# Attention heads in pairs on different rows and columns of the PE array, with a pair's transposes in two PSUM banks

## The chip, the cores and the metric

One core of a Trainium2 chip runs the whole program. The metric is the device time of one execution in microseconds (us); lower is better. TensorE is called PE here, VectorE DVE, ScalarE ACT, GpSimd POOL, and SP issues the loads of weights.

## What is computed

One sequence of 256 tokens with 1024 features goes through two kinds of layers, two of each. The first kind is an FFN, a mixer and an FFN; the mixer has 8 NSA query heads in 2 groups that share keys and values (three branches each: compressed blocks, selected blocks, a window), and 8 MoBA heads. At this length the selected blocks and the window both come to causal attention over all 256 keys. The second kind is a hybrid mixer (8 sparse heads, 4 differential heads) and an FFN. All heads have 64 features. The core of the mixer, cut:

```python
for l in range(DEPTH):
    x = x + 0.5 * swiglu(rms_norm(x, norm_ffn1[l]), ...)
    x = x + hybrid_mixer(rms_norm(x, norm_mix[l]), w_in[l], ...)
    x = x + 0.5 * swiglu(rms_norm(x, norm_ffn2[l]), ...)

def nsa_mixer(q, k_cmp, v_cmp, k_slc, v_slc, k_win, v_win, gates, ...):
    ...
    p_w = masked_softmax(s_w, valid_w)
    o_win = jnp.einsum('bgrcqk,bgckd->bgrcqd', p_w, vw)
    return g[..., 0:1] * o_cmp + g[..., 1:2] * o_slc + g[..., 2:3] * o_win
...
return jnp.concatenate([o_nsa, o_moba], axis=-1) @ w_out
```

The differential heads take `softmax(q0 k0) - lam * softmax(q1 k1)` times v; the sparse heads have a mask from an indexer that keeps 64 keys a query.

## The kernel before

Every projection is a float32 product made of three passes (lines 201 to 206, `mm3`): both operands are split into a high and a low part, weights by ACT and DVE (L183, L184) in chunks of 1 MB. Eight PSUM banks are shared by tag: four `acc` (projections, and the sums of `to_residual`, which takes all four), two `S` (`psS`, scores), one `T` (`psT`, transposes), one `O` (`psO`, outputs). A planner takes the program's instructions by their place in it: on each engine it issues the earliest one whose operands and bank it holds to be ready, so that products of a later projection run between those of the heads. PE then works through that order and waits where an operand is late.

An attention stage works on two heads at a time (a pair). `scores_exp` (L361 to 383) makes, for one head after the other in a bank of its own: the scores of the late 128 queries with 256 keys (L371), those of the early ones with 128 keys (L372), and two products with a bfloat16 identity that add the mask (L373, L374); then DVE takes a maximum (L377) and ACT an exponential with its sum (L380), twice a head. `attend` (L399 to 413) scales the probabilities (L405, L406) and then, for one head after the other, makes three transposes into the one `psT` bank (L389 to 391, `p_T`), copies them to SBUF (ACT for the first head, L394, DVE for the second, L396) and makes the two products with the values into 64 of the rows of `psO` (L412, L413). A float32 product with the heads' operands goes to PE as two instructions.

The mixer (L432 to 571) has this program order: the projection of keys and values, windows, queries, `moba_in(0)` (MoBA's queries), the compressed branch (`cmp_probs`), then `nsa(k)` for k = 0 to 3 (two `attend` each, and a product with the compressed values, L533), `moba_in(1)`, the transposes of MoBA's queries (`heads_T`, L350), `moba_in(2)`, the transposes of its keys, `moba(k)` four times, and `to_residual` with `w_out` (L242 to 246). NSA's pair is two query heads of one group, both on the same 64 rows; MoBA's pair is two heads on rows 0 to 63 and 64 to 127.

The hybrid (L816 to 1116) goes: indexer, queries, keys, the differential queries, `av`, then `sparse(k)` four times (L1007), the projection of the differential keys (`xc`), `bv`, `diff(h)` four times (L1019; it has `scores_exp` and one `p_T`, and products L1034 to 1036), the gates' products (`gate`, L964) into `acc`, and the up-projections.

Of the kernel before, what the change touches and what calls it, by code (L numbers as in the profile page):

```python
# [9 lines left out]
F32 = mybir.dt.float32  # L10
# [10 lines left out]
D = 1024  # L21
# [11 lines left out]
class K:  # L33
    """One core's program: two macaron layers (NSA and MoBA mixer), then two layers of the
    sparse and differential hybrid. Tokens lie on partitions in the residual and in the
    attention inputs, features on partitions where a product contracts them."""
# [6 lines left out]
    # ---------------------------------------------------------------- set-up  # L43
# [49 lines left out]
    def loads(self):  # L93
        """What later stages want from DRAM beside their weights."""
# [25 lines left out]
    def more_consts(self):  # L120
# [3 lines left out]
        self.caus = cp.tile([128, 128], BF16, name="caus")  # L124
# [3 lines left out]
            pattern=[[-1, 128]], channel_multiplier=1,  # L128
# [61 lines left out]
    # ---------------------------------------------------------------- norms  # L190
    def rstd_of(self, ms, n, tag):
        """(ms / n + EPS) ** -0.5"""
        nc = self.nc
        w = ms.shape[-1]
        v = self.small(w, tag + "v")
        nc.gpsimd.tensor_scalar(v, ms, 1.0 / n, EPS, op0=ALU.mult, op1=ALU.add)
        r = self.small(w, tag + "r")
        nc.gpsimd.tensor_tensor(r, v, self.neghalf[:, 0:w], op=ALU.pow)
        return r

    def mm3(self, out, ah, al, bh, bl, start, stop):
        """out += (ah + al).T @ (bh + bl); al.T @ bl lies below float32's own rounding."""
# [5 lines left out]
    def behind(self, ins):  # L208
        """What is traced within queues behind these instructions, each on its engine."""
# [10 lines left out]
    def ft(self):  # L220
        """A bank for a tile of features; leaves the accumulators of to_residual alone."""
# [3 lines left out]
    # ------------------------------------------------ products to the residual  # L225
    def to_residual(self, yh, yl, w, nk, scale, after, held=2):
        """x += scale * y @ w, y with features on partitions (yh(k), yl(k): [128, 256]). The early
        tokens end first, and after(t, n) is told of each piece of x."""
# [20 lines left out]
        for c in range(nch):  # L249
            hl = self.weights(  # L250
                w[c * 256 : (c + 1) * 256, :].rearrange("(j p) n -> p j n", p=128), [2, D]
            )
# [12 lines left out]
    # ------------------------------------------------------------------ FFN  # L265
# [77 lines left out]
    def heads_T(self, pool, src, name, scale=None):  # L343
        """src [128, 2, 512] (8 heads of 64) -> [128, 4, 256]: two heads on each column of tiles."""
# [16 lines left out]
    def scores_exp(self, pool, qk, masks):  # L361
        """Two heads: exp(s - max) [128, 2, 384] (late queries first), sums [128, late or early x head]."""
        nc = self.nc
        m1, m0 = masks
# [3 lines left out]
        for i, (q, k) in enumerate(qk):  # L368
            ps = self.psS()
            w = m1.shape[-1]  # L370
            nc.tensor.matmul(ps[:, 0:256], q[:, 128:256], k[:, 0:256], start=True, stop=False)  # L371
            nc.tensor.matmul(ps[:, 256:384], q[:, 0:128], k[:, 0:128], start=False, stop=False)  # L372
            nc.tensor.matmul(ps[:, 256 - w : 256], self.identb, m1, start=False, stop=False)  # L373
            nc.tensor.matmul(ps[:, 256:384], self.identb, m0, start=False, stop=True)  # L374
            for t, c0, c1 in ((0, 0, 256), (1, 256, 384)):
                j = 2 * t + i
                nc.vector.tensor_reduce(  # L377
                    nm[:, j : j + 1], ps[:, c0:c1], axis=AX.X, op=ALU.max, negate=True
                )
                nc.scalar.activation(  # L380
                    p[:, i, c0:c1], ps[:, c0:c1], AF.Exp, bias=nm[:, j : j + 1], accum_out=sm[:, j : j + 1]
# [3 lines left out]
    def p_T(self, pool, p, eng):  # L385
        """[128, 384] -> keys on partitions: [k0 x q0 | k0 x q1 | k1 x q1]"""
        nc = self.nc
        ps = self.psT()
        nc.tensor.transpose(ps[:, 0:128], p[:, 256:384], self.ident)  # L389
        nc.tensor.transpose(ps[:, 128:256], p[:, 0:128], self.ident)  # L390
        nc.tensor.transpose(ps[:, 256:384], p[:, 128:256], self.ident)
        pt = pool.tile([128, 384], F32, tag="PT", name="PT", bufs=3)
        if eng == 0:
            nc.scalar.copy(pt, ps[:, 0:384])  # L394
        else:
            nc.vector.tensor_copy(pt, ps[:, 0:384])  # L396
        return pt

    def attend(self, pool, o, qk, vs, masks, coef, start, stop):  # L399
        """o [2 heads x 64, 256] += softmax(q k) v, rows weighted by what coef makes of the sums."""  # L400
        nc = self.nc
        p, sm = self.scores_exp(pool, qk, masks)
        c = coef(sm)
        for i in range(2):
# [26 lines left out]
    # ------------------------------------------------------------ first mixer  # L431
    def mixer(self, l, pr, after):  # L432
# [3 lines left out]
        with tc.tile_pool(name="mix", bufs=1) as mp, ExitStack() as es:  # L436
# [13 lines left out]
            vcb = mp.tile([128, 2, 256], F32, name="vcb")  # L450
# [51 lines left out]
            caus = (self.caus, self.caus)  # L502

            def gated(h, i):
                def coef(sm):
# [3 lines left out]
                    cv = c.rearrange("p (t h) -> p t h", t=2)  # L509
                    gv = gt.rearrange("p t (h i) -> p t h i", i=3)  # L510
                    for t in (1, 0):
                        nc.vector.tensor_tensor(
                            cv[:, 1 - t, :], cv[:, 1 - t, :], gv[:, t, h : h + 2, i], op=ALU.mult
# [10 lines left out]
            def nsa(k):  # L524
                g = k // 2
                gs = slice(64 * g, 64 * g + 64)
                o = self.psO()
                for i, v in ((1, kv[:, :, 384 + 64 * g : 448 + 64 * g]), (2, kw[:, :, 128 + 64 * g : 192 + 64 * g])):
                    qk = [(qrT[gs, (2 * k + j) % 4, :], kT[i - 1][gs, :]) for j in range(2)]
                    vs = [[v[:, t, :] for t in range(2)]] * 2  # L530
                    self.attend(mp, o, qk, vs, caus, gated(2 * k, i), start=i == 1, stop=False)
                kk = (2 * k) % 4
                nc.tensor.matmul(  # L533
                    o[:, 0:256], vcb[:, g, kk * 64 : kk * 64 + 128], pcT[:, g, :], start=False, stop=True
# [786 lines left out]
```

## Time and profile before

| | us |
|---|---|
| median of three runs | 1950.57 (1947.41 to 1956.95) |
| span of the profiled execution | 1950.2 |
| the profiled execution's own time | 1950.2 (its span; no other time stands for it) |
| PE busy | 1906.6 (98%), 12336 matrix instructions |
| PE weight loads | 1676.6 (86%), beside the products |
| DVE busy | 1250.6 (64%) |
| ACT busy | 922.4 (47%) |
| POOL busy | 327.1 (17%) |
| chain that ended last | PE 90%, DVE 5%, POOL 2% |
| a 1 MB chunk of weights, from issue to landing | 4.8 to 5.1 (medians by weight) |

The ends of PE's instructions are modelled, and each lasts longer than it holds the array up, so that PE reads as busy almost throughout. What an instruction costs a stretch without gaps is the distance from its start to the next one's.

### The profile page before, as it was taken

What the parts mean: (1) busy time and instruction counts of PE and PEld (TensorE: products, weight loads), DVE (VectorE), ACT (ScalarE), POOL (GpSimd) and SP (SyncE); (2) the same over time, 40 slices, a digit from 0 to 9 for tenths busy, and PEclk for the clock granted to TensorE, in tenths of its full rate; (3) what the DMA queues carried; (4) which work ended last, traced back from release to release, by engine and by line L of the source; (5) the groups of instructions that cost most, each with busy time, mean ns of one, the idle gap of its engine ahead of it and who ended that gap; (6) DMA issues with size and microseconds to landing.
All of it is one profiled execution on the core that took longest, in us unless ns stands there. A gap on an engine that the chain in (4) does not pass through costs nothing.

```text
span 1950.2 us, 30625 instructions
## 1 busy us (share of the span) xinstructions
PE 1906.6 (98%) x12336; PEld 1676.6 (86%) x12336; DVE 1250.6 (64%) x2138; ACT 922.4 (47%) x1664; POOL 327.1 (17%) x360
## 2 busy tenths in 40 slices
PE   8999999999999999999999998999999989999999
PEld 8998776899899988767999775899998767999997
DVE  6764475665657655666666487766765696666662
ACT  6553354544445444445444453545444534545442
POOL 4110120011102101100111154000210351011110
PEclk9999999999999999899999998999999999999999
DMA  8545452354655364612546443355546532355552
GB/s 277 191 166 186 163 204 68 108 174 152 216 183 185 130 237 153 216 44 87 177 162 224 157 140 108 109 178 189 174 137 215 191 115 104 124 179 174 173 194 88
DMA packets 149023, 314.63 MB, mean 161 GB/s; under 512 B 5525, under 2 KB 30257, under 8 KB 148881
## 3 DMA queue, kind: packets, MB, share of 16 engines
q1 hardware_dynamic: 147952, 311.15, 47.0%
q0 software_dynamic: 896, 1.52, 0.4%
q8 instruction: 97, 1.59, 0.3%
q14 instruction: 46, 0.37, 0.1%
q10 hardware_dynamic: 32, 0.01, 0.0%
HBM read 311.61 MB, written 1.05 MB: 160 GB/s over the span
## 4 chain that ended last, share of the span: by engine, by line
PE 90%; DVE 5%; POOL 2%; issue 1%; DMA 1%; ACT 1%; SPq 0%; POOLq 0%; ACTq 0%; DVEq 0%
PE acc L205 12%; PE acc L206 12%; PE acc L204 11%; PE acc L243 8%; PE acc L246 8%; PE acc L242 8%; PE psS L204 3%; PE psS L205 3%; PE psS L206 3%; PE psS L371 3%; PE psT L204 2%; PE psT L206 2%; PE psT L205 2%; PE psO L412 2%; PE psO L204 1%; PE psO L206 1%
## 5 line engine op out<-in xcount | busy, mean ns | idle before, releaser
L184 DVE TENSOR_TENSOR lo<-raw,hi 128x1024 fp32r<-128x1024 f32 (+1 forms) x604 | 708.8, 1197 | 374.1 <-ACT hi L183 372.6
L183 ACT ACTIVATE hi<-raw 128x1024 fp32r<-128x1024 f32 (+1 forms) x604 | 584.6, 1007 | 458.5 <-PE acc L205 134.0
L205 PE MATMUL acc<-xl,hi 128*128 128x256 f32 x1408 | 400.2, 285 | 0.0
L204 PE MATMUL acc<-xh,hi 128*128 128x256 f32 x1408 | 399.2, 285 | 0.0
L206 PE MATMUL acc<-xh,lo 128*128 128x256 f32 x1408 | 398.7, 284 | 0.0
L205 PEld LDWEIGHTS acc<-xl,hi 128*128 128x128 f32 x1408 | 271.0, 192 | 0.4
L204 PEld LDWEIGHTS acc<-xh,hi 128*128 128x128 f32 x1408 | 270.3, 193 | 0.5 <-ACT xh L1222 0.2
L206 PEld LDWEIGHTS acc<-xh,lo 128*128 128x128 f32 x1408 | 270.0, 192 | 0.0
L312 POOL TENSOR_TENSOR hh<-sg,gu 128x256 f32<-128x256 f32 x132 | 139.0, 1059 | 650.5 <-DVE sg L308 626.4
L243 PE MATMUL acc<-lo,gh 128*128 128x512 f32 x528 | 210.7, 399 | 0.0
L242 PE MATMUL acc<-hi,gh 128*128 128x512 f32 x528 | 208.4, 395 | 0.0
L205 PE MATMUL acc<-lo,xh 128*128 128x512 f32 (+2 forms) x416 | 164.6, 396 | 13.9 <-DVE lo L184 13.9
L246 PE MATMUL acc<-hi,gl 128*128 128x512 f32 x528 | 173.9, 396 | 0.0
L204 PE MATMUL acc<-hi,xh 128*128 128x512 f32 (+2 forms) x416 | 163.3, 396 | 2.4 <-ACT ix L854 1.9
L206 PE MATMUL acc<-hi,xl 128*128 128x512 f32 (+2 forms) x416 | 162.3, 392 | 2.7 <-DVE xl L1223 2.7
L204 PE MATMUL psS<-xh,hi 128*128 128x256 f32 x480 | 136.6, 285 | 0.0
L206 PE MATMUL psS<-xh,lo 128*128 128x256 f32 x480 | 136.0, 283 | 0.0
L205 PE MATMUL psS<-xl,hi 128*128 128x256 f32 x480 | 136.0, 283 | 0.0
L217 ACT ACTIVATE gh<-hh 128x256 fp32r<-128x256 f32 x132 | 55.2, 418 | 149.2 <-POOL hh L312 149.0
L243 PEld LDWEIGHTS acc<-lo,gh 128*128 128x128 f32 x528 | 99.5, 188 | 23.8
L246 PEld LDWEIGHTS acc<-hi,gl 128*128 128x128 f32 x528 | 99.4, 188 | 23.3
L242 PEld LDWEIGHTS acc<-hi,gh 128*128 128x128 f32 x528 | 99.3, 188 | 22.5
(408 smaller groups left out, 3343.5 us busy)
## 6 DMA issues: line engine op xcount, KB each, us to landing
raw<-in_w_in_dram SPq DMA_DIRECT2D x60, 1024.0 KB, 5.0
raw<-in_w_ffn_down_dram SPq DMA_DIRECT2D x44, 1024.0 KB, 4.8
raw<-in_w_ffn_up_dram SPq DMA_DIRECT2D x40, 1024.0 KB, 5.0
raw<-in_w_ffn_in_dram SPq DMA_DIRECT2D x40, 1024.0 KB, 5.1
raw<-in_w_ffn_gate_dram SPq DMA_DIRECT2D x39, 1024.0 KB, 5.0
raw<-in_w_ffn_out_dram SPq DMA_DIRECT2D x22, 1024.0 KB, 4.8
raw<-in_w_out_dram SPq DMA_DIRECT2D x16, 1024.0 KB, 4.8
raw<-in_w_ffn_gate_dram SPq DMA_DIRECT2D x10, 512.0 KB, 3.6
```

Source lines behind the costliest of these rows:

```text
L183: nc.scalar.activation(hi[:, hs], raw[:, hs], AF.Copy),
L184: nc.vector.tensor_tensor(lo[:, hs], raw[:, hs], hi[:, hs].bitcast(F32), op=ALU.subtract),
L204: mm(out, ah, bh, start=start, stop=False)
L205: mm(out, ah, bl, start=False, stop=False)
L206: self.last = mm(out, al, bh, start=False, stop=stop)
L217: nc.scalar.activation(hi, src, AF.Copy)
L242: mm(accs[t][n], ah, hi[:, j, cs], start=k == 0, stop=False)
L243: mm(accs[t][n], ah, lo[:, j, cs], start=False, stop=False)
L246: mm(accs[t][n], al, hi[:, j, cs], start=False, stop=k == nk - 1)
L312: nc.gpsimd.tensor_tensor(hh, sg, gu[:, 1, :], op=ALU.mult)
L371: nc.tensor.matmul(ps[:, 0:256], q[:, 128:256], k[:, 0:256], start=True, stop=False)
L412: nc.tensor.matmul(oo, vs[i][0], pt[:, 0:256], start=start, stop=False)
```

## The change

Scores: a pair's two products with 256 keys follow each other, then its two with 128 keys, then one mask product a head, 256 wide (`caus` holds the triangle twice) or 384 wide (the sparse mask). Transposes: `p_T` takes both heads; the two transposes of a head that belong to the first 128 keys go to `psT`, the one of the later keys to a bank of tag `acc`; ACT copies the first bank, DVE the second. Values: the heads' products alternate in the same way. NSA's pairs become head r of group 0 and head r of group 1, so that they lie on different rows, and with that the compressed values, the gates' coefficients and the order in which `w_out` is loaded (two transfers of 64 partitions a chunk, for NSA's two chunks) change. `PT` has two buffers of a pair in place of three of a head. The number of banks of each tag stays, and so does the program order of projections and stages.

```diff
-        self.caus = cp.tile([128, 128], BF16, name="caus")
+        self.caus = cp.tile([128, 256], BF16, name="caus")
...
     def wraw(self, src, shape, pieces=1):
         t = self.wp.tile([128] + shape, F32, tag="raw", name="raw", bufs=3)
+        if isinstance(src, list):
+            for ps_, part in src:
+                self.nc.sync.dma_start(t[ps_], part)
+            return t
...
-        for i, (q, k) in enumerate(qk):
-            ps = self.psS()
-            w = m1.shape[-1]
-            nc.tensor.matmul(ps[:, 0:256], q[:, 128:256], k[:, 0:256], start=True, stop=False)
-            nc.tensor.matmul(ps[:, 256:384], q[:, 0:128], k[:, 0:128], start=False, stop=False)
-            nc.tensor.matmul(ps[:, 256 - w : 256], self.identb, m1, start=False, stop=False)
-            nc.tensor.matmul(ps[:, 256:384], self.identb, m0, start=False, stop=True)
+        w = mask.shape[-1]
+        ps = [self.psS() for _ in qk]
+        for b, (q, k) in zip(ps, qk):
+            nc.tensor.matmul(b[:, 0:256], q[:, 128:256], k[:, 0:256], start=True, stop=False)
+        for b, (q, k) in zip(ps, qk):
+            nc.tensor.matmul(b[:, 256:384], q[:, 0:128], k[:, 0:128], start=False, stop=False)
+        for b in ps:
+            nc.tensor.matmul(b[:, 384 - w : 384], self.identb, mask, start=False, stop=True)
...
-    def p_T(self, pool, p, eng):
+    def p_T(self, pool, p, n):
...
+        k0, k1 = self.psT(), self.acc()
+        pt = pool.tile([128, n, 384], F32, tag="PT", name="PT", bufs=2)
+        for i in range(n):
+            nc.tensor.transpose(k0[:, 256 * i : 256 * i + 128], p[:, i, 256:384], self.ident)
+            nc.tensor.transpose(k0[:, 256 * i + 128 : 256 * i + 256], p[:, i, 0:128], self.ident)
+        nc.scalar.copy(pt[:, :, 0:256], k0[:, 0 : 256 * n].rearrange("p (i q) -> p i q", i=n))
+        for i in range(n):
+            nc.tensor.transpose(k1[:, 128 * i : 128 * i + 128], p[:, i, 128:256], self.ident)
+        nc.vector.tensor_copy(pt[:, :, 256:384], k1[:, 0 : 128 * n].rearrange("p (i q) -> p i q", i=n))
         return pt
...
-        for i in range(2):
-            pt = self.p_T(pool, p[:, i, :], i)
-            oo = o[64 * i : 64 * i + 64, 0:256]
-            nc.tensor.matmul(oo, vs[i][0], pt[:, 0:256], start=start, stop=False)
-            nc.tensor.matmul(oo[:, 128:256], vs[i][1], pt[:, 256:384], start=False, stop=stop)
+        pt = self.p_T(pool, p, 2)
+        oo = [o[64 * i : 64 * i + 64, 0:256] for i in range(2)]
+        for i in range(2):
+            nc.tensor.matmul(oo[i], vs[i][0], pt[:, i, 0:256], start=start, stop=False)
+        for i in range(2):
+            nc.tensor.matmul(oo[i][:, 128:256], vs[i][1], pt[:, i, 256:384], start=False, stop=stop)
...
-            def nsa(k):
+            def nsa(r):
...
+                gs = [slice(64 * g, 64 * g + 64) for g in range(2)]
+                for i, v, c0 in ((1, kv, 384), (2, kw, 128)):
+                    qk = [(qrT[h, r, :], kT[i - 1][h, :]) for h in gs]
+                    vs = [[v[:, t, c0 + 64 * g : c0 + 64 * g + 64] for t in range(2)] for g in range(2)]
+                    self.attend(mp, o, qk, vs, self.caus, gated(r, i), start=i == 1, stop=False)
...
-        for g in range(2):
-            for m in range(2):
-                nc.tensor.matmul(
-                    ps[:, 64 * g : 64 * g + 64], zr[:, m, g].rearrange("p r n -> p (r n)"), w2[1][:, m, :],
-                    start=m == 0, stop=m == 1,
-                )
+        for m in range(2):
+            nc.tensor.matmul(
+                ps[:, 0:64], zr[:, m].rearrange("p u g n -> p (u g n)"), w2[1][:, m, :],
+                start=m == 0, stop=m == 1,
+            )
```

## Rows read from the trace of the kernel before

**Rows 1.** The page, part 1: engine, busy us, share of the span, instructions.

```profile
PE 1906.6 (98%) x12336; PEld 1676.6 (86%) x12336; DVE 1250.6 (64%) x2138; ACT 922.4 (47%) x1664; POOL 327.1 (17%) x360
```

**Rows 2.** Windows: length, busy PE, PEld, DVE, ACT, POOL; PEclk, DMA, GB/s.

```profile
260.06:361.50 101.44, 100.66 (x504) 67.92 (x503) 65.41 (x184) 47.80 (x136) 11.90 (x12) 1.00 0.27 95
811.83:906.40 94.57, 93.64 (x481) 64.84 (x479) 63.92 (x181) 45.57 (x134) 8.67 (x8) 1.00 0.26 90
267.95:325.20 57.25, 57.25 (x288) 37.18 (x287) 37.30 (x117) 28.79 (x86) 4.15 (x4) 1.00 0.24 87
...
1194.89:1225.40 30.51, 30.51 (x153) 21.24 (x153) 23.86 (x59) 16.71 (x47) 8.61 (x7) 1.00 0.25 81
1233.86:1257.00 23.14, 23.14 (x169) 20.35 (x168) 16.31 (x51) 13.43 (x48) 0.00 (x0) 1.00 0.27 91
1605.24:1677.60 72.36, 70.93 (x411) 55.46 (x410) 50.11 (x123) 35.95 (x104) 8.54 (x7) 0.95 0.30 101
```

**Rows 3.** Timeline of PE, indexer, first hybrid: start, us, line, operation.

```profile
1148.07 0.70 PE L919 MATMUL psS<-iT 64*128 64x256 f32 x4
1148.70 0.50 PE L205 MATMUL acc<-lo,xh 128*128 128x512 f32 x1
...
1150.05 0.70 PE L919 MATMUL psS<-iT 64*128 64x256 f32 x2
1150.67 0.50 PE L204 MATMUL acc<-hi,xh 128*128 128x512 f32 x1
```

**Rows 4.** The same view, the first MoBA pair of the first mixer.

```profile
334.04 0.69 PE L371 MATMUL psS<-mT 64*128 64x256 f32 x2
...
334.89 0.23 PE L373 MATMUL psS<-caus,identb 128*128 128x128 bf16 x1
...
340.94 0.27 PE L389 MATMUL psT<-ident,P 128*128 128x128 f32 x1
...
342.06 0.65 PE L412 MATMUL psO<-PT,m 128*64 128x256 f32 x2
...
342.86 0.33 PE L389 MATMUL psT<-ident,P 128*128 128x128 f32 x1
```

**Rows 5.** By source line, count, duration ns, first and last start; POOL by time.

```profile
264.59 1.60 POOL L429 TENSOR_TENSOR m<-r,r 128x256 f32<-128x256 f32 x1
...
L350 PE MATMUL psT<-ident,m x32: 269/273/300, 328.3 to 878.7; 128*128 128x128 f32 x32
...
L391 PE MATMUL psT<-ident,P x72: 271/273/422, 276.9 to 1677.5; 128*128 128x128 f32 x72
```

**Rows 6.** Groups on PE, windows 260.06:325.2, 325.2:361.6 and 1233.86:1257.

```profile
L204 PE MATMUL acc<-hi,xh 128*128 128x512 f32 x32 | 12.9, 404 | 0.0
...
L242 PE MATMUL acc<-hi,oh 128*128 128x512 f32 x22 | 8.9, 404 | 0.0
...
L204 PE MATMUL acc<-xh,hi 128*128 128x256 f32 x30 | 9.0, 301 | 0.0
```

**Rows 7.** Timeline of PE, two products of moba_in(1) in a dense stretch.

```profile
262.22 0.39 PE L204 MATMUL acc<-hi,xh 128*128 128x512 f32 x1
262.44 0.39 PE L205 MATMUL acc<-lo,xh 128*128 128x512 f32 x1
```

**Rows 8.** Groups by line on DVE and ACT, 267.95 to 325.2.

```profile
L184 DVE TENSOR_TENSOR lo<-raw,hi 128x1024 fp32r<-128x1024 f32 x9 | 11.2, 1249 | 0.4 <-ACT hi L183 0.3
...
L380 ACT ACTIVATE P<-psS,nm 128x256 f32<-128x256 f32 (+1 forms) x32 | 13.4, 421 | 5.6 <-DVE nm L377 4.9 <-DVE c L507 0.5
```

**Rows 9.** Windows, columns as in rows 2, an idle stretch and what follows.

```profile
1177.30:1187.80 10.50, 0.85 (x5) 0.39 (x3) 8.33 (x20) 0.00 (x0) 6.51 (x5) 0.75 0.22 70
1187.80:1192.80 5.00, 5.00 (x15) 4.02 (x16) 3.67 (x9) 2.09 (x3) 0.00 (x0) 0.50 0.86 287
```

**Rows 10.** Timeline of DVE: evacuation of `xc`, and its last rotary product.

```profile
1205.95 0.74 DVE L852 TENSOR_SCALAR tok<-acc,r 128x512 f32<-128x512 f32 x1
...
1219.23 0.68 DVE L814 TENSOR_TENSOR tok<-t,hr 128x512 f32<-128x512 f32 x1
```

More of the change, by code (lines that the diff above doesn't have):

```diff
@@ L249, in to_residual @@
         for c in range(nch):
-            hl = self.weights(
-                w[c * 256 : (c + 1) * 256, :].rearrange("(j p) n -> p j n", p=128), [2, D]
-            )
+            src = w(c) if callable(w) else w[c * 256 : (c + 1) * 256, :].rearrange("(j p) n -> p j n", p=128)
+            hl = self.weights(src, [2, D])
             if c < nch - held:
@@ L359, in heads_T, with scores_exp @@
         return dst
-    def scores_exp(self, pool, qk, masks):
+    def scores_exp(self, pool, qk, mask):
         nc = self.nc
-        m1, m0 = masks
         p = pool.tile([128, 2, 384], F32, tag="P", name="P", bufs=2)
@@ L377, in scores_exp, with attend @@
                 nc.vector.tensor_reduce(
-                    nm[:, j : j + 1], ps[:, c0:c1], axis=AX.X, op=ALU.max, negate=True
+                    nm[:, j : j + 1], b[:, c0:c1], axis=AX.X, op=ALU.max, negate=True
                 )
                 nc.scalar.activation(
-                    p[:, i, c0:c1], ps[:, c0:c1], AF.Exp, bias=nm[:, j : j + 1], accum_out=sm[:, j : j + 1]
+                    p[:, i, c0:c1], b[:, c0:c1], AF.Exp, bias=nm[:, j : j + 1], accum_out=sm[:, j : j + 1]
                 )
         return p, sm
-    def p_T(self, pool, p, eng):
+    def p_T(self, pool, p, n):
         nc = self.nc
[L388 to L396, printed above, removed]
+        k0, k1 = self.psT(), self.acc()
[7 more added lines that the diff above has]
+        nc.vector.tensor_copy(pt[:, :, 256:384], k1[:, 0 : 128 * n].rearrange("p (i q) -> p i q", i=n))
         return pt
-    def attend(self, pool, o, qk, vs, masks, coef, start, stop):
+    def attend(self, pool, o, qk, vs, mask, coef, start, stop):
         nc = self.nc
-        p, sm = self.scores_exp(pool, qk, masks)
+        p, sm = self.scores_exp(pool, qk, mask)
         c = coef(sm)
@@ L500, in moba_in, with gated @@
                 return m
-            caus = (self.caus, self.caus)
-            def gated(h, i):
+            def gated(r, i):
                 def coef(sm):
@@ L541, in moba @@
                 vs = [[mv[:, t, (2 * k + j) * 64 : (2 * k + j) * 64 + 64] for t in range(2)] for j in range(2)]
-                self.attend(mp, o, qk, vs, caus, plain, start=True, stop=True)
+                self.attend(mp, o, qk, vs, self.caus, plain, start=True, stop=True)
                 self.split(oh[:, 4 + k, :], ol[:, 4 + k, :], o[:, 0:256])
@@ L568, in mixer, with out_rows @@
                 moba(k)
-            self.to_residual(
-                lambda k: oh[:, k, :], lambda k: ol[:, k, :], a["w_out"][l], KT, 1.0, after, held=1
-            )
+            w_out = a["w_out"][l]
+            def out_rows(c):
+                if c >= 2:
+                    return w_out[c * 256 : (c + 1) * 256, :].rearrange("(j p) n -> p j n", p=128)
+                return [
+                    (slice(64 * g, 64 * g + 64), w_out[256 * g + 128 * c : 256 * g + 128 * c + 128, :]
+                     .rearrange("(j d) n -> d j n", d=64))
+                    for g in range(2)
+                ]
+            self.to_residual(lambda k: oh[:, k, :], lambda k: ol[:, k, :], out_rows, KT, 1.0, after, held=1)
     def cmp_blocks(self, mp, l, kv, flats):
@@ L659, in compress @@
         ps = self.psS()
-        zr = mp.tile([128, 2, 2, 4, 32], F32, tag="c2", name="zr")
+        zr = mp.tile([128, 2, 2, 2, 32], F32, tag="c2", name="zr")
         nc.gpsimd.memset(zr, 0.0)
@@ L706, in cmp_probs @@
         nc.vector.reciprocal(c, c)
[L707 to L709 removed]
+        c4 = c.rearrange("p (t r g) -> p t r g", t=2, r=4)
+        g5 = gt.rearrange("p t (g r i) -> p t r g i", g=2, r=4)
+        pc = cp.tile([128, 2, 8, 32], F32, tag="c2", name="pc")
         nc.gpsimd.memset(pc, 0.0)
```

54 lines of the change are left out of this document (21 added, 33 removed).

## The prediction

> **What bounds the kernel now.** I read the page first: PE is busy 98% of the span [rows 1], so what matters is PE's time and every moment in which PE would find nothing to do. Then the windows of the four kinds of attention stages [rows 2]: PE is busy throughout in all of them and holds the full clock (1.00), while DVE is busy two thirds of NSA's window (37.3 of 57.25 us). PE is full there because the planner puts products of later projections between those of the heads. From the first product of `moba_in(1)` at 260.06 to the end of NSA's transposes, 96 such products ran (three lines of 32), and then 72 of `to_residual` beside MoBA's heads (three lines of 21 or 22, and seven earlier ones) [rows 6]. Beside the four differential pairs there were 89 of the gates, three lines of about 30, after 23 that ran just ahead of them [rows 6]. So the heads' chain (scores, maximum, exponential, scaling, transpose, copy, value product) is hidden behind products that need neither its results nor its banks. Whether that stays so decides this case.
>
> **The change part by part.**
>
> *Scores and values in pairs.* A head's scores hold PE for 0.85 us up to the mask (334.04 to 334.89), its value products for 0.80 (342.06 to 342.86) [rows 4]. That two halves of the array work side by side is in the trace: in the indexer two products on different row halves, four instructions back to back, take 0.63 us (1148.07 to 1148.70), and one alone takes 0.62 [rows 3]. So the second head can come free. There are 40 pairs (16 NSA, 8 MoBA, 8 sparse, 8 differential), 32 of them with paired values. At most the change takes off 40 x 0.85 = 34 us of scores and 32 x 0.80 = 25.6 us of values, and at most 4 us of masks (80 heads, one product fewer each, some 0.05 us). For the scores this needs both `psS` banks free at once; they come free one head after the other, as the exponentials end, so half of the 34 is the better guess. All of it counts only while PE is what a stage waits for.
>
> *Transposes and copies.* Their number stays. ACT copies 512 columns in place of 384, DVE 256 in place of 384; the sum is about the same, and I cost it at nothing.
>
> *The second bank is an `acc`.* This is the part that costs. The planner hands out the banks of a tag in the order of the program, whether or not an earlier taker is ready. The trace shows it: MoBA's queries were rotated by POOL's last step at 264.59 (1.60 us), so their transposes could have run from 266.2. They first ran at 328.3, after all sixteen transposes of NSA's heads in that one `psT` bank (first at 276.9), which stand ahead of them in the program [rows 5]. Products of `moba_in(2)`, which stand behind them in the program but use another tag, ran in between. Now each pair's later-key transposes take an `acc`, and every projection that today fills the gaps takes its `acc` banks behind them in program order: `moba_in(1)` and `moba_in(2)` behind NSA's eight, `to_residual` behind MoBA's four, `xc` and `bv` behind the sparse four, the gates behind the differential four. They can't start before the last pair of the stage ahead has its transposes on PE. So PE runs a stage with the heads alone, waits on DVE and ACT in it, and does the fillers afterwards.
>
> A stage's new length: the first pair takes as long as today up to its transposes, 9.0 us for NSA (267.95 to 276.9) [rows 2, 5] and 6.9 for MoBA (334.04 to 340.94) [rows 4]; I use 9.0 for the sparse heads too, 6.9 for the differential ones. Each later pair takes a cycle. From below it is bounded by DVE: 37.3 us less nine weight splits of 11.2 in NSA's window is 26.1, over eight pairs 3.3 us [rows 2, 8] (ACT's 32 exponentials alone are 13.4 us, 1.7 a pair [rows 8]). From above by today's cycle, (325.2 - 276.9) / 7 = 6.9; for the sparse pairs (30.5 - 9.0) / 3 = 7.2, for the differential ones (23.1 - 6.9) / 3 = 5.4 [rows 2]. PE no longer makes a pair wait, but two score banks, one `psT` and one `psO` still make one pair wait for another; neither end is nearer, so I take the middle: 5.1, and 4.4 for the differential ones. Stages: NSA 9.0 + 7 x 5.1 = 44.7, MoBA 22.2, sparse 24.3, differential 6.9 + 3 x 4.4 = 20.1.
>
> Fillers, dense: 0.23 us each (262.22 to 262.44, rounded) [rows 7], half of that for the gates' 256 columns.
>
> First mixer, from 260.06: 7.9 us that `moba_in(1)` fills today up to the first score, 44.7 NSA, then `moba_in(1)` (48 x 0.23 = 11) and about 7 for its evacuation, rotation and transposes (my estimate; `moba_in(2)` lies beside it and beside MoBA's first chain), 22.2 MoBA, 72 x 0.23 = 16.8 of `to_residual`: 109.6, against 101.4 today [rows 2], +8.2. Second mixer: 48 products of `to_residual` and otherwise the same, 104.0 against 94.6 [rows 2], +9.4.
>
> First hybrid, from 1194.89: 24.3 sparse, `xc` 11, some 12.5 for its norm and rotation (today 13.9, 1205.95 to 1219.9, with DVE shared [rows 10]) and the keys' transposes, with `bv` beside them, 20.1 differential, 112 gate products x 0.12 = 13.4: 81.3 against 62.1 (1194.89 to 1257) [rows 2], +19.2. Second hybrid: 139 gate products, 84.6 against 72.4 [rows 2], +12.2.
>
> *The rest.* Half the products for the compressed values and four fewer DVE steps a layer, about 1 us in all. `w_out`'s first chunks come as two transfers of 64 partitions on SP's queue; the cover is that `to_residual` now starts later than they land, and without it, the most is one chunk's landing a layer, about 5 us. Wider `caus`, POOL once: nothing. `PT` with two pair buffers: nothing, since `psT` is freed later.
>
> Sum: 8.2 + 9.4 + 19.2 + 12.2 - 1 = +48 us on the profiled span of 1950.2, which stands 0.4 below the median of 1950.57: 1998.
>
> *A rule of the skill.* In 1177.3 to 1187.8 PE was nearly idle; in the next 5.0 us its clock was 0.50, the 1.2 GHz level [rows 9]. Fifteen products took that time, 0.33 each at best, where the full clock needs 0.23: each such restart costs about 2 us. The Trainium skill, "TensorE: Matmul & The Clock Gate", section "Loop structure matters more than you think", says that a loop which makes PE wait before every product runs its products cold, at half rate. The trace agrees for the one long wait; for a row of short ones no row here shows it. By the rule the stages would run at half clock, which is the third rival.
>
> **The rivals.**
>
> *The fillers keep running.* If the planner let a later projection take a free `acc` ahead of the heads, PE would stay full and the change would give what it is made for: 25.6 of values, 17 to 34 of scores, up to 4 of masks, so 1887 to 1908; I take 1905. For it: three of four `acc` banks would stand free. Against it: the transposes that waited 62 us in line [rows 5]. It decides from the first filler that starts within a stage. Chance 0.13.
>
> *DVE's floor.* With PE out of the way the cycle falls to 3.3 us. Then NSA takes 32.1, MoBA 16.8, sparse 18.9, differential 16.8: -9.8 and -8.6 for the mixers, +10.5 and +3.5 for the hybrids, in all 1945 or, with splits of weights in between, up to 1965: no change that can be told. For it: ACT and DVE are far from full. Against: one bank for transposes, two for scores. Chance 0.10.
>
> *Half clock in the stages.* A pair holds PE some 2.8 us (0.85 scores, 0.25 masks and change of rows, 0.65 for six transposes, 0.80 values, 0.25 again); at half clock as much again, and the cycle is back at today's 6.9, 7.2 and 5.4: +26, +27, +28 and +21, so 2053. For it: [rows 9]. Against: the clock held 1.00 wherever PE was fed [rows 2]. Chance 0.15.
>
> **How the numbers follow.** The forecast, 1998 (1965 to 2030 with its cycle between 4 and 6), has 0.60; with the three above 0.98, and 0.02 for something else. The range runs from the floor to the half clock, 1945 to 2050, and leaves out the rival below it and the upper edge. A measurement of this kernel tells about 0.5% (9.8 us) from no change. Faster is the first rival and a sliver of the floor: 0.14. Same is most of the floor: 0.08. Slower is the rest: 0.78.
>
> **What would show it.** Right: between the first scores and the last transposes of a stage, no product of `moba_in(1)`, `to_residual`, `xc` or the gates; PE well under full there, waiting for DVE and ACT; the dense products in one block behind; NSA's stage some 45 us long; a pair's value products in 0.8 us. The clock column then tells between forecast and half clock. Wrong: fillers within the stages, or stages of some 32 us with fillers behind them.

## The result, and the profile after

The changed kernel takes 2041.7 us (median of 2036.95 to 2047.6), the kernel before 1950.9 beside it: a ratio of 1.046, 95% interval 1.044 to 1.048, some 91 us more. The profiled execution of after spans 2038.1 us, 88 more than that of before. The forecast was 1998, the range 1945 to 2050: slower, as forecast, and for the reason given, but by nearly twice the sum. It lies above the 1965 to 2030 that the forecast gave its own cycle, and within the range because that ran on to the half clock.

The page of after, part 1, its columns as in [rows 1]:

```profile
PE 1906.6 (94%) x12248; PEld 1686.6 (83%) x12248; DVE 1254.1 (62%) x2134; ACT 927.0 (45%) x1668; POOL 326.2 (16%) x360
```

PE is busy for as long as before (1906.6 us), in 88 us more of span: by this view alone, all the loss is time in which PE stood idle. But an instruction's busy time is longer at a lower clock, so the windows have to be read. The eight attention stages of after, first score to last transpose, in program order (first and second mixer: NSA, MoBA; first and second hybrid: sparse, differential); columns as in [rows 2]:

```profile
264.81:312.40 47.59, 35.08 (x192) 23.33 (x192) 31.99 (x111) 22.07 (x77) 3.69 (x4) 0.78 0.27 67
339.77:365.20 25.43, 18.90 (x89) 13.21 (x90) 14.27 (x48) 9.92 (x38) 0.00 (x0) 0.59 0.12 41
838.37:879.70 41.33, 31.45 (x193) 21.40 (x192) 26.13 (x107) 19.98 (x75) 0.00 (x0) 0.83 0.17 45
907.03:929.55 22.52, 15.20 (x89) 10.75 (x90) 14.28 (x48) 9.89 (x38) 0.00 (x0) 0.81 0.15 47
1228.41:1253.90 25.49, 19.67 (x90) 12.46 (x90) 14.97 (x46) 9.78 (x38) 1.21 (x1) 0.63 0.26 83
1282.53:1307.55 25.02, 19.04 (x72) 14.52 (x73) 16.11 (x52) 10.05 (x47) 0.00 (x0) 0.50 0.29 106
1669.58:1694.70 25.12, 16.74 (x90) 10.45 (x90) 16.01 (x51) 10.00 (x39) 0.29 (x1) 0.75 0.26 88
1722.53:1747.55 25.02, 18.74 (x72) 14.29 (x73) 16.12 (x52) 10.06 (x47) 0.00 (x0) 0.51 0.29 109
```

Three things are to be seen against [rows 2]. PE ran 192 instructions in NSA's first stage where there were 288, and 72 in the differential one where there were 169. It stood idle in every stage: lengths less busy time, over the eight, come to 237.5 - 174.8 = 62.7 us, where the same stages of before come to 280.5 - 279.0 = 1.4. And its clock, 1.00 in seven of the eight stages of before and 0.91 in the other, lies between 0.50 and 0.83; 0.50 is the 1.2 GHz level. Over the whole span the time at that level is some 206 us, and 41 before. Of the stages of before, the one with 0.91 and the sum over all eight:

```profile
1605.24:1644.30 39.06, 37.63 (x170) 26.39 (x170) 28.43 (x66) 17.84 (x48) 8.54 (x7) 0.91 0.37 130
...
sum 280.47, PE 279.04 PEld 198.90 DVE 191.43 ACT 141.10 POOL 24.61; mean PE 34.88 PEld 24.86 DVE 23.93 ACT 17.64 POOL 3.08
```

What is missing are the products of later projections. The groups of PE in NSA's first stage (columns: busy us, mean ns | idle time before them, and what ended most of it):

```profile
L374 PE MATMUL psS<-kt,qrT 64*128 64x256 f32 x32 | 10.5, 534 | 5.5 <-ACT P L385 4.8 <-DVE qrT L361 0.7
L400 PE MATMUL acc<-ident,P 128*128 128x128 f32 x16 | 5.6, 352 | 3.0 <-DVE P L411 2.8
...
L418 PE MATMUL psO<-PT,kv 128*64 128x256 f32 x16 | 3.1, 469 | 2.6 <-ACT PT L398 2.6
...
L208 PE MATMUL acc<-hi,xh 128*128 128x512 f32 x1 | 0.5, 481 | 0.0
L209 PE MATMUL acc<-lo,xh 128*128 128x512 f32 x1 | 0.5, 478 | 0.0
```

Two products of `moba_in(1)` (L208, L209) are left in a stage that had 67 projection products and seven of `to_residual`; the other stages of after have one or two each, where 38 to 102 ran. PE now waits for the heads' own chain: scores for the exponential that frees their bank, transposes for the scaled probabilities, values for the copy. Right behind the stage (312.5 to 339.7) the rest of the 96 products stands in one block (a product that runs across 312.5 is counted in both views):

```profile
L210 PE MATMUL acc<-hi,xl 128*128 128x512 f32 x32 | 12.7, 397 | 0.0
L209 PE MATMUL acc<-lo,xh 128*128 128x512 f32 x32 | 12.6, 393 | 0.0
L208 PE MATMUL acc<-hi,xh 128*128 128x512 f32 x31 | 12.2, 395 | 0.0
```

The pairs do what the change says. PE's timeline of after, the last values of NSA and the first scores of MoBA:

```profile
313.47 0.65 PE L418 MATMUL psO<-PT,kw 128*64 128x256 f32 x4
...
314.27 0.70 PE L537 MATMUL psO<-pcT,vcb 128*128 128x256 f32 x2
...
339.71 0.70 PE L374 MATMUL psS<-mT 64*128 64x256 f32 x4 [0.79 <-DVE mT L361]
...
340.56 0.52 PE L378 MATMUL psS<-caus,identb 128*128 128x256 bf16 x2
```

Both heads' values take 0.80 us (313.47 to 314.27) and both heads' scores 0.85 (339.71 to 340.56), what one head took before [rows 4]. So the gain is there, and the loss comes from elsewhere.

### The profile page after: what moved, and what is told of

Its sections match the earlier page's. It is cut to its first block, busy times and chain, and to the rows that moved or that the text cites. A ratio compares the mean times of both kernels' runs of the same rounds, so it can differ in the third digit from the quotient of the medians.

```text
span 2038.1 us, 30439 instructions
## 1 busy us (share of the span) xinstructions
PE 1906.6 (94%) x12248; PEld 1686.6 (83%) x12248; DVE 1254.1 (62%) x2134; ACT 927.0 (45%) x1668; POOL 326.2 (16%) x360
## 4 chain that ended last, share of the span: by engine, by line
PE 84%; DVE 7%; ACT 4%; POOL 3%; issue 1%; DMA 1%; SPq 0%; POOLq 0%; ACTq 0%; DVEq 0%
PE acc L208 11%; PE acc L210 11%; PE acc L209 11%; PE acc L247 8%; PE acc L250 7%; PE acc L246 7%; PE psS L208 3%; PE psS L210 3%; PE psS L209 3%; DVE lo L188 3%; PE psT L208 2%; PE psT L209 2%; PE psT L210 2%; ACT P L385 2%; PE psS L374 2%; PE psO L208 1%
## 5 line engine op out<-in xcount | busy, mean ns | idle before, releaser
L209 PE MATMUL acc<-xl,hi 128*128 128x256 f32 x1408 | 400.3, 285 | 0.0
L208 PE MATMUL acc<-xh,hi 128*128 128x256 f32 x1408 | 399.6, 285 | 0.0
L209 PEld LDWEIGHTS acc<-xl,hi 128*128 128x128 f32 x1408 | 271.7, 193 | 0.2
L208 PEld LDWEIGHTS acc<-xh,hi 128*128 128x128 f32 x1408 | 271.4, 193 | 0.2
L208 PE MATMUL acc<-hi,xh 128*128 128x512 f32 (+2 forms) x416 | 162.4, 392 | 2.5 <-ACT ix L867 2.0
L209 PE MATMUL acc<-lo,xh 128*128 128x512 f32 (+2 forms) x416 | 160.8, 387 | 0.0
L208 PE MATMUL psS<-xh,hi 128*128 128x256 f32 x480 | 136.4, 284 | 0.0
L209 PE MATMUL psS<-xl,hi 128*128 128x256 f32 x480 | 135.8, 283 | 0.0
```

The costliest lines, as they stand in the source:

```text
L208: mm(out, ah, bh, start=start, stop=False)
L209: mm(out, ah, bl, start=False, stop=False)
```

## The experiments

The theory: the `acc` bank in the heads' line takes the later projections out of the stages. The rivals: the pairing itself costs, or the half clock does, or the order of the steps between the stages. Each time stands with its ratio to the kernel before and the 95% interval.

### One psT bank again

In the changed kernel, `p_T`:

```diff
-        k0, k1 = self.psT(), self.acc()
+        k0 = self.psT()
...
+        k1 = self.psT()
         for i in range(n):
             nc.tensor.transpose(k1[:, 128 * i : 128 * i + 128], p[:, i, 128:256], self.ident)
```

> The changed kernel, with the transposes of a pair's later keys in the one psT bank again (behind the copy of the first part) in place of an acc bank; all else stays paired. Bank theory: the products of later projections come back into the stages (some 50 to 70 in NSA's, 40 in MoBA's, 90 and more in the differential ones), PE is full there, and the time falls by 95 to 150 us to between 1890 and 1945. Rival, the pairing itself costs (alternating rows, the half clock that comes with it, or the longer chain of a pair): the stages stay empty of other products or PE still waits in them, and the time stays between 2025 and 2045.

Measured: 1922.2 us, 0.985 (0.983 to 0.988): 119 us less than the changed kernel for one bank's tag, and 1.5% faster than the kernel before. Its NSA, MoBA, sparse and differential stages of the first mixer and hybrid:

```profile
265.06:316.40 51.34, 50.43 (x282) 32.72 (x282) 39.65 (x119) 28.96 (x87) 6.26 (x7) 1.00 0.45 123
324.25:349.50 25.25, 25.05 (x141) 16.95 (x141) 16.72 (x50) 14.37 (x44) 0.00 (x0) 1.00 0.27 87
1177.72:1206.05 28.33, 28.19 (x146) 18.75 (x146) 25.24 (x60) 17.26 (x47) 9.64 (x7) 1.00 0.34 115
1214.26:1237.95 23.69, 23.62 (x187) 21.65 (x185) 17.36 (x53) 14.21 (x52) 0.00 (x0) 1.00 0.33 102
```

and `moba_in(1)` and `moba_in(2)` in NSA's window of this kernel:

```profile
L208 PE MATMUL acc<-hi,xh 128*128 128x512 f32 x30 | 13.1, 436 | 0.0
L210 PE MATMUL acc<-hi,xl 128*128 128x512 f32 x30 | 12.4, 415 | 0.0
L209 PE MATMUL acc<-lo,xh 128*128 128x512 f32 x30 | 12.4, 414 | 0.0
```

90 products are back in the stage, PE is full and the clock is 1.00. The pairing stayed as it was, so it is not what costs, and the half clock is a consequence of the empty stages.

### The kernel before with an acc bank

In the kernel before, `p_T`, no pairing:

```diff
-        ps = self.psT()
+        ps = self.acc() if eng else self.psT()
```

> The kernel before, with one word changed: the second head's transposes go into an acc bank in place of psT (in the differential stages, every other head's). No pairing. Bank theory: the projections' acc banks now stand in line behind the heads, the stages of NSA, MoBA and the sparse heads run without products of later projections, and the time rises by 40 to 100 us to between 1990 and 2050. Rival, one more bank for transposes only helps and the loss came from the pairs: 1940 to 1955.

Measured: 2076.2 us, 1.062 (1.058 to 1.067): the loss comes without any pair, and larger than I expected by 26 us at least. NSA's and the differential stage of the first layers:

```profile
265.65:310.90 45.25, 40.90 (x208) 26.91 (x207) 27.39 (x107) 19.86 (x76) 0.00 (x0) 0.89 0.09 35
...
1295.63:1322.25 26.62, 22.99 (x79) 16.11 (x79) 15.03 (x49) 10.83 (x46) 0.00 (x0) 0.51 0.28 100
```

One projection product was left in each stage. The two runs together, the bank taken from the pairs and given to single heads, show the cause from both sides. The trace is that of the fastest of four executions (2060; the others took 2075 to 2078). That the time is 34 us above the changed kernel's (2076 against 2042) fits a gain of the pairs even in empty stages, but the two also differ in how the transposes are shared out, so the size of that gain is not shown.

### The acc bank in the differential stages alone

In the kernel with one psT bank:

```diff
-        k1 = self.psT()
+        k1 = self.acc() if n == 1 else self.psT()
```

> The kernel with the later keys' transposes in psT (1922), but with the acc bank back in the eight differential attends alone. Bank theory: the gates' 107 to 116 products leave the two differential stages (23.5 us, then some 25 at half clock) and follow them (13 us), so that each loses 13 to 15 us: 1948 to 1955; the other six stages keep their products. Rival, one stage kind alone is too short to matter, since the gates' products have enough other work beside them: 1920 to 1930.

Measured: 1965.6 us, 1.007 (1.004 to 1.009), 43 above the kernel with one psT bank; 26 to 33 were expected. Its first sparse and first differential stage:

```profile
1172.30:1200.70 28.40, 28.28 (x147) 18.82 (x146) 25.28 (x60) 17.10 (x47) 9.51 (x7) 1.00 0.35 113
1208.81:1233.85 25.04, 19.37 (x73) 14.79 (x73) 14.03 (x50) 10.07 (x47) 0.00 (x0) 0.50 0.13 43
```

Only the stages with the `acc` bank emptied; the sparse one beside them is as in the kernel with one psT bank. So the effect goes stage by stage. Where the time went the trace shows: the two differential stages are only 1.3 and 1.9 us longer than in the kernel with one psT bank, but from the first one's last transpose to the next sparse score it takes 362.8 us in place of 345.6, and from the second one's to the end 290.7 in place of 270.2. So what follows the stages, the gates' products first, costs 17 and 20 us, where 13 had been expected. The lower clock lasts some 5 us beyond each stage; whether that makes up the excess no run shows.

### A second bank of another tag

In the kernel with one psT bank:

```diff
-        k1 = self.psT()
+        k1 = self.psS()
```

> The changed kernel with the later keys' transposes in one of the two psS banks in place of an acc bank: still two banks for a pair's transposes, but the second one of a tag that only the heads use in the stages. If it is the acc's place in line that costs, and not the second bank, the later projections' products stay within the stages and the time is near the 1922 of the single psT bank, 1915 to 1945 (a pair now takes three turns in two psS banks, which can lengthen its cycle). Rival, any second bank drives the other products out or starves PE: above 1990.

Measured: 1992.5 us, 1.023 (1.020 to 1.027). The time is the rival's (above 1990), 70 us above the single psT bank, and by the second half of its text: PE starves. Its first half fails: the projections' products stayed in the stages (89 of `moba_in` and 36 of `to_residual` in NSA's first), as the theory of the place in line says. The window of NSA's stage, and of its groups the transposes of the later keys:

```profile
264.47:337.65 73.18, 64.14 (x315) 44.97 (x315) 46.38 (x123) 32.98 (x89) 5.41 (x7) 0.89 0.40 116
```

```profile
L401 PE MATMUL psS<-ident,P 128*128 128x128 f32 x16 | 5.0, 322 | 9.0 <-DVE P L412 9.0
```

The stage grew from 51 to 73 us: the next pair's scores stand in line for psS behind these transposes, which wait for the scaled probabilities, so that one pair's chain follows the other's. There were more products of projections in it than in the 51 us, and PE still waited 9 us. I read this as the same rule of the line, with the heads themselves as those who wait. So it is the `acc` tag that empties the stages, and not a second bank as such; that a second bank is harmless is not shown, and in this tag it costs.

### Work for PE while a pair waits

In the changed kernel, behind a pair's scores:

```diff
+        dm = self.acc()
+        for j in range(12):
+            nc.tensor.matmul(dm[:, 0:256], self.identb, self.caus, start=True, stop=True)
         return p, sm
```

> The changed kernel with 12 products of the bfloat16 identity with the wide triangle added a pair, into an acc bank that nobody reads, so that PE has work while a pair waits. If half the clock is what makes the differential stages 25 us in place of the forecast 20, the granted clock in the stages goes back to near 1.00, the differential stages fall to 20 to 21, NSA's first to about 42, and the time falls by 15 to 30 us to 2010 to 2027. Rival, the stages wait for DVE, ACT and the banks whatever the clock: the clock rises, the stages keep their length within 1 us or grow by the added products (1.3 us a pair at full clock), and the time is between 2035 and 2075.

Measured: 2021.3 us, 1.036 (1.034 to 1.038), 20 us less than the changed kernel though PE has 480 products more to do. NSA's and MoBA's stage in the first mixer, and the first differential stage:

```profile
259.21:308.00 48.79, 40.62 (x276) 28.13 (x275) 32.20 (x111) 22.22 (x77) 3.56 (x4) 0.90 0.28 65
335.36:357.80 22.44, 19.07 (x124) 13.59 (x125) 14.37 (x48) 9.93 (x38) 0.00 (x0) 0.85 0.14 47
...
1271.84:1292.42 20.58, 15.65 (x109) 11.90 (x110) 15.76 (x53) 10.56 (x47) 0.00 (x0) 0.92 0.36 133
```

With the clock at 0.92 both differential stages are 20.6 us long in place of 25.0, and MoBA's 22.4 and 20.1 in place of 25.4 and 22.5, though more is done in them. So half the clock is what made the short stages longer than the forecast. NSA's stages grew (48.8 and 48.3 from 47.6 and 41.3; 42 had been expected of the first): there what the clock gave back went to the added products or was never the limit, which this run leaves open.

The 20 us, though, are mostly not from the stages: the eight together are 4 us shorter. Of the 19.4 us by which the profiled span fell, 13.4 lie ahead of NSA's first scores, which start at 259.3 in place of 264.8 in the first mixer and 465.3 us behind the first MoBA stage in place of 473.2 in the second. The first pair's added products run there as well, ahead of its scores, and the clock is higher. The stretch ahead of the first NSA stage, in the changed kernel and in this one:

```profile
236.67:264.75 28.08, 25.86 (x153) 20.43 (x152) 17.19 (x38) 12.42 (x17) 3.24 (x6) 0.82 0.67 225
```

```profile
235.76:259.28 23.52, 21.95 (x164) 17.39 (x160) 17.45 (x38) 12.54 (x17) 3.50 (x7) 1.00 0.80 269
```

Three of the added products lie within that stretch and nine at its end; whether they kept the clock up is not shown.

### The keys' transposes first, and then the first scores too

In the changed kernel (in the hybrid likewise, `bkT` ahead of `bv`):

```diff
-            mv = moba_in(2)
             mk = self.heads_T(mp, mks, "mT")
+            mv = moba_in(2)
```

> The changed kernel, with two lines of the program order exchanged in each layer: the transposes of MoBA's keys stand ahead of moba_in(2), those of the differential keys ahead of bv. The order theory: the gap between NSA's last transpose and MoBA's first score falls from 27.4 us to some 18, the gap sparse to differential from 28 to some 22, and the time falls by 9 a mixer and 5 a hybrid to about 2013 (2005 to 2025). Rival, the rotation's chain on DVE and POOL is what the gap waits for: gaps within 2 us of 27 and 28, time 2035 to 2045; or the products that left the gap come back ahead of the first values and the stage grows by as much: gap 18, time 2035 to 2045.

Measured: 2057.1 us, 1.055 (1.052 to 1.057): 15 us slower than the changed kernel, outside all three texts. PE's timeline:

```profile
327.91 0.66 PE L353 MATMUL psT<-ident,m 128*128 128x128 f32 x4 [2.02 <-POOL m L436]
...
329.77 1.06 PE L353 MATMUL psT<-ident,m 128*128 128x128 f32 x4
330.48 0.78 PE L210 MATMUL acc<-hi,xl 128*128 128x512 f32 x1
...
338.90 0.39 PE L210 MATMUL acc<-hi,xl 128*128 128x512 f32 x1
339.22 0.70 PE L374 MATMUL psS<-mT 64*128 64x256 f32 x4
```

PE waited 2.0 us for the rotation, the keys were transposed by 330.5, 8 us earlier than in the changed kernel, and then the rest of `moba_in(2)` ran through to 339.2 before MoBA's first score, which had been ready since about 331.5. The products stand ahead of the scores in the program and were always ready, so they went first. The gap stayed (29.0 us, from NSA's last transpose at 310.2). The 15 us lie elsewhere: MoBA's stages took 29.2 us each, where the changed kernel has 25.4 and 22.5, with PE waiting up to 3.7 us for an exponential, and the gaps of the hybrids 32.3 and 31.7, where it has 28.6 and 27.9, with one wait of 4.9 us in the first.

The run that tests this reading moves the first scores as well:

```diff
             mk = self.heads_T(mp, mks, "mT")
+            pre = moba_scores(0)
             mv = moba_in(2)
```

> As e3 (keys' transposes ahead of moba_in(2), and ahead of bv), with one more step moved: MoBA's first pair has its scores, maxima and exponentials ahead of moba_in(2) in program order. In e3 all 48 products of moba_in(2) ran between the rotation and the first score, although the keys stood transposed at 331. If place in the program alone decides between ready products, the first score now runs at some 331 (7 to 8 us earlier after NSA's last transpose), the rest of moba_in(2) runs beside the first pair's maxima and exponentials, and each mixer loses 6 to 10 us: 2037 to 2045 against the 2057 of e3. Rival, the first values wait for moba_in(2) anyhow and the stage grows by what the gap lost: 2053 to 2061.

Measured: 2048.0 us, 1.050 (1.047 to 1.054), 9 us less than with the keys alone; the expectation was 12 to 20, so it lies between the two texts. The first score now follows the keys' transposes at once:

```profile
333.27 1.05 PE L353 MATMUL psT<-ident,m 128*128 128x128 f32 x4
335.25 0.70 PE L374 MATMUL psS<-mT 64*128 64x256 f32 x4
```

The gap fell from 29.0 to 22.8 us in the first mixer and from 27.4 to 23.0 in the second, and 30 products of `moba_in(2)` ran within MoBA's stage. The place in the program decides, then, as read. It doesn't pay: the gaps of the mixers are 4.5 us shorter than in the changed kernel, but MoBA's stages took 29.5 and 28.9 us and the gaps of the hybrids 32.2 and 32.3, and the whole stays above it.

### Which pairing gives what

Three kernels with `p_T` as in the kernel before (a head's three transposes into psT): all else paired; of the values and scores, the scores alone in pairs; the values alone.

```diff
...
+        for i in range(n):
+            ps = self.psT()
+            nc.tensor.transpose(ps[:, 0:128], p[:, i, 256:384], self.ident)
+            nc.tensor.transpose(ps[:, 128:256], p[:, i, 0:128], self.ident)
+            nc.tensor.transpose(ps[:, 256:384], p[:, i, 128:256], self.ident)
...
```

> The changed kernel with the transposes as before (a head's three into the one psT bank, copied by ACT for the first head and by DVE for the second); scores, masks and values stay paired. Bank theory: with no acc bank in the heads' line it comes out near the kernel with the later keys' transposes in psT (1922), 1905 to 1930, with 50 or more products of later projections in NSA's stages. Rival, the two-part transposes themselves give the gain over the kernel before (fewer, wider copies): 1935 to 1955.

From this kernel to the one with the scores alone in pairs (`attend`, and `p_T` taking one head):

```diff
-        pt = self.p_T(pool, p, 2)
...
         for i in range(2):
-            nc.tensor.matmul(oo[i], vs[i][0], pt[:, i, 0:256], start=start, stop=False)
-        for i in range(2):
-            nc.tensor.matmul(oo[i][:, 128:256], vs[i][1], pt[:, i, 256:384], start=False, stop=stop)
+            self.p_T(pool, p, [i], pt)
+            oo = o[64 * i : 64 * i + 64, 0:256]
+            nc.tensor.matmul(oo, vs[i][0], pt[:, i, 0:256], start=start, stop=False)
+            nc.tensor.matmul(oo[:, 128:256], vs[i][1], pt[:, i, 256:384], start=False, stop=stop)
```

> As the run with per-head transposes (e5), but a head's two value products stand right behind its own transposes, as before, so that only the scores alternate. If two value products on different columns share the array's time, they lose 0.3 to 0.8 us in each of 32 pairs: 10 to 25 us above e5, so 1925 to 1950. Rival, the second head's products fall into the wait for its copy in any case: within 6 us of e5.

and to the one with the values alone (`scores_exp`):

```diff
         for b, (q, k) in zip(ps, qk):
             nc.tensor.matmul(b[:, 0:256], q[:, 128:256], k[:, 0:256], start=True, stop=False)
-        for b, (q, k) in zip(ps, qk):
             nc.tensor.matmul(b[:, 256:384], q[:, 0:128], k[:, 0:128], start=False, stop=False)
-        for b in ps:
             nc.tensor.matmul(b[:, 384 - w : 384], self.identb, mask, start=False, stop=True)
```

> As e5, but a head's scores and mask stand together, as before, so that only the value products alternate. If the scores run side by side (0.85 us a head before), this loses 0.4 to 0.85 us in each of 40 pairs: 16 to 34 us above e5, 1930 to 1955. Rival, the two banks come free one after the other, so that the scores hardly overlap in e5: within 6 us of e5.

Measured: 1928.3 (0.988; 0.985 to 0.990), 1936.0 (0.992; 0.988 to 0.995) and 1935.7 (0.992; 0.989 to 0.995). The first is within its expectation. The other two are 7 to 8 us above it, between their two texts, and their intervals overlap with its own, so the times don't separate scores from values. The trace says why so little is at stake. In the first kernel, NSA's stage:

```profile
286.72 0.65 PE L419 MATMUL psO<-PT,kv 128*64 128x256 f32 x2
287.30 0.70 PE L374 MATMUL psS<-kt,qrT 64*128 64x256 f32 x2
...
288.14 0.43 PE L419 MATMUL psO<-PT,kv 128*64 128x256 f32 x1
288.15 0.43 PE L421 MATMUL psO<-PT,kv 128*64 128x128 f32 x2
...
290.31 0.70 PE L374 MATMUL psS<-kt,qrT 64*128 64x256 f32 x2
```

The scores come as x2, one head: by their order in the stage those at 287.30 are the first head's of the fifth pair, and the other head's follow 3.0 us later (290.31). The planner issues a product as soon as its own bank is free, and the pair falls apart. So do the values, whose first head (286.72) is ready 1.4 us before the second (288.14); only the first head's products with 128 queries are left to run beside the second's (288.15).

The table gives for each kernel how many pairs have both heads' first scores, or first values (four instructions), on PE with nothing between them. It also gives what the scores, values and masks of all pairs take on PE, each instruction counted from its start to the next one's, waits left out. Both are worked out from the traces.

| kernel | pairs together: scores | values | us: scores | values | masks |
|---|---|---|---|---|---|
| before | 0 of 40 | 0 of 32 | 71.5 | 51.2 | 11.8 |
| all paired, a head's transposes together | 11 | 0 | 54.4 | 44.7 | 6.1 |
| scores alone | 19 | 0 | 50.9 | 51.6 | 5.9 |
| values alone | 1 | 0 | 70.3 | 43.1 | 7.3 |
| one psT bank | 13 | 32 | 54.6 | 30.6 | 6.4 |

The run that was to pair the values alone has no pair of values together, so none of the three shows what paired values are worth. Only in the kernel with one psT bank, where a pair's copies end together, are they all together: they take 14 us less on PE than in the first of the three (30.6 against 44.7), and the time is 6 us less. Pairs written side by side in the program are side by side on PE only where both become ready together.

## Why the prediction was right, and what it mis-sized

*The mechanism* held, step by step. The stages ran without the later projections but for one or two products each [rows 5, 6 against the groups of after], with PE waiting for ACT and DVE, and the products followed in a block. The tag of one bank is the cause: taking it away gives 1922, adding it to the kernel before 2076.

*The first rival* (the fillers keep running, 1905) had the value of the pairs about right on PE: 17 to 34 us for scores, 25.6 for values and up to 4 for masks had been allowed, and by the table above the kernel with one psT bank takes 17, 21 and 5 us less than the kernel before. Its time fell by 28 to 31 us only (1922), since by the same count projections (8 us), transposes (2) and idle time (6) took some of it back.

*The stages' lengths.* NSA: 47.6 and 41.3, forecast 44.7. MoBA 25.4 and 22.5, forecast 22.2. Sparse 25.5 and 25.1, forecast 24.3. The cycle taken from the middle of two far bounds, 5.1, came out as 5.5 and 4.6 in NSA ((47.6 - 9.0) / 7 and (41.3 - 9.0) / 7); DVE's floor of 3.3 was nowhere. The differential stages were the miss: 25.0 both, forecast 20.1, at a clock of 0.50 and 0.51; with the clock at 0.92 they took 20.6. So 4.4 of the 4.9 us each go with the clock.

*The gaps.* This was the term that failed: that `moba_in(2)` "lies beside it and beside MoBA's first chain", and `bv` beside the hybrid's rotation. From NSA's last transpose to MoBA's first score it took 27.4 and 27.3 us, where the sum had 18; from the sparse to the differential stage 28.6 and 27.9, where it had 23.5. In the mixers nearly all of the 96 products at 0.23 us (22 us) stand in that gap with the evacuation and the transposes behind them. The rotated keys were there at about 330.0, and their transposes ran at 336.47 and 338.27:

```profile
328.38 1.60 POOL L436 TENSOR_TENSOR m<-r,r 128x256 f32<-128x256 f32 x1
```

```profile
336.47 0.60 PE L353 MATMUL psT<-ident,m 128*128 128x128 f32 x4
338.27 0.66 PE L353 MATMUL psT<-ident,m 128*128 128x128 f32 x4 [1.20 <-ACT mT L359]
```

By the planner's rule, the earliest ready one by its place in the program, a product that is always ready and stands ahead of a chain doesn't run beside it but before it. I had used that rule for the banks and not for the engine. The two runs with the steps moved show it at work in the mixers; in the hybrids the moved step made the gap longer, so what its 5 us are made of is not shown.

The missing 40 us (88 on the profiled span, 48 forecast), by terms: 9.4 + 9.3 for the gaps in the mixers, 5.1 + 4.4 in the hybrids, 4.9 + 4.9 for the differential stages, 3.2 + 0.3 for MoBA's, 1.2 + 0.8 for the sparse ones, 2.9 - 3.4 for NSA's: 43. Ahead of NSA's first score it was 3.2 us less (264.8, where the sum had 268.0), and what stands behind the stages (`to_residual`, the gates) came within 2 us of each term.

*The third rival*, half clock in the stages, came true in part. Its total, 2053, lies nearer to 2041.7 than the forecast does, but mostly for another reason: it made every stage as long as before, NSA's 57 us and the sparse ones 30, and they were 41 to 48 and 25. The clock was 0.50 in the differential stages and 0.59 to 0.83 in the others, and the gaps at full clock made up the rest. Its own terms, besides, give a cycle of 5.1 + 2.8 = 7.9, and it used 6.9. The half clock came with short waits: PE's longest one in the first differential stage was 2.5 us. The rule of the Trainium skill that stood beside it ("TensorE: Matmul & The Clock Gate", section "Loop structure matters more than you think") speaks of a long wait before every product, 8 us in its example; here the clock fell with shorter and fewer ones, so the trace goes beyond it. PE's waits there, by its line and what it waited for (us in total, times, longest; the one for bkT ended as the stage began):

```profile
PE acc L400 <- DVE P L1039: 2.5, 1, 2.5
PE psS L374 <- ACT P L385: 2.1, 1, 2.1
PE psS L374 <- DVE bkT L361: 2.0, 1, 2.0
PE psO L1045 <- ACT PT L398: 1.4, 3, 0.5
```

*The restart* of [rows 9] was read from a mean over unlike products: some of the fifteen were transposes of 128 columns, and those of 512 columns stood 0.43 us apart (1188.34 to 1188.77), not 0.33. No term of the sum used it.

*The rest.* The two transfers a chunk of `w_out`, the wider `caus` and `PT` in two buffers show no cost of their own: the kernel with one psT bank has them all and is faster than the kernel before. No run took them one by one.

## What to carry to other kernels

Before a step gets a bank of a tag that others share, write down who takes that tag behind it in program order: what used to fill the gaps may stand there, and a full engine is then worth more than the edit itself saves. Work that is always ready runs at its place in the program, so it hides a chain only if it stands behind that chain's first step. Operations meant to run side by side have to become ready together, or the planner pulls them apart.

## What the runs showed of the hardware that was not expected

PE's clock fell to 0.50 in stages whose waits are short: in the first differential stage PE was busy 19.0 of 25.0 us, with no wait over 2.5 us, and had 0.50 throughout. Twelve small products a pair that nobody reads brought it to 0.92 and the stage to 20.6 us. The kernel became 20 us faster by doing more, though most of that lies ahead of NSA's stages.

Four products on two halves of the columns (two heads' values with 64 columns each) take as long as two on one half, 0.80 us, as do scores on two halves of the rows, 0.85. The trace of before had shown it for rows alone [rows 3].
